# Token slots of 2112 bytes that start 64 bytes apart modulo 1024, and half the scratch for dynamic transfers

## The chip, the cores and the metric

The kernel runs on one core of one Trainium2 chip. The metric is device time in microseconds: the median of three runs, lower is better. Profile rows name the engines as PE (TensorE matmuls), PEld (TensorE weight loads), DVE (VectorE), ACT (ScalarE), POOL (GpSimd) and SP (SyncE, which issues most transfers).

## What is computed

Two transformer blocks on 256 tokens of width 2048, all in float32. The first block has two layers, each over the tokens `x` and (in layer 0, and for keys and values in layer 1) 256 context tokens:

```
hx = rmsnorm(x, norm_g[l]) * (1 + scale) + shift          # scale, shift, gate = silu(c) @ w_mod[l] + b_mod[l]
q, k, v, g_att, u_pool, g_pool, a, b, g_conv = split(hx @ w_in[l])
y  = concat(attention(q, k, v) * silu(g_att), pooling(u_pool) * silu(g_pool), conv(a, b) * silu(g_conv)) @ w_out[l]
x  = x + gate * y
```

The second block is `h @ w_in_2`, block attention, a state-space branch (64 groups of 16 channels, 64 states each) with its own `w_glu_2`, two merged branches through `w_out_2`, and a gated feed-forward part of 5632 hidden channels: `up = causal_conv3(h2 @ w_up_2)`, `x + g2 * ((silu(gt) * val) @ w_down_2)`. The output is 256 by 2048.

## The kernel before, in words

**Arithmetic.** Every large matrix product is made of three TensorE matmuls in the type float32r: each operand is split into a high part that float32r holds exactly and a low part that is the rest, and the product is high times high, high times low and low times high. All of these go through `mm` (line 152) and appear as L153. Transposes (`tr`, L159) and the small products of attention, state space and modulation are float32 matmuls, their outputs are named `sd`; outputs of the large products are named `mm`.

**Weights.** A weight chunk is 512 rows by 512 columns, 1 MB. SP loads it into a buffer `wr` (three of them, 8 KB of each partition, four k tiles of 512 columns); `_split_job` (line 352) turns it into `wh` by ACT (L168) and `wl` by DVE (L172), two buffers each. Modulation weights go through four buffers `mv` of 4 KB per partition, and in the start phase through token slots (line 852, 128 loads of 256 KB).

**Token slots.** Nearly every other tile is a token slot: `S()` (line 76) gives one of 61 buffers with tag `s`, 512 elements of 4 bytes in each partition, 2048 bytes. Split activations lie in them (high part in the first 1024 bytes and low part in the second, or one slot each), and so do attention's scores, evacuated products, rows of constants, and the pieces that POOL's queue loads and stores. `MV()`, `mid()` (tag `m`, 512 bytes), `small()` (tag `c8`) and `const()` give the other tiles.

**Who is stationary.** `chunk_a` (line 407) keeps 128 columns of a weight chunk stationary and streams the token slot past them (256 columns, or 512 in layer 0); `chunk_b` (line 384) keeps 128 tokens of a slot stationary and streams 512 weight columns. In `chunk_b` token block 0 is the slice that starts at byte 0 of the slot's half, block 1 the slice at byte 512; in `chunk_a` the stationary slice starts at byte 512 n of a 2048-byte row of the weight buffer, n from 0 to 3, and the stream at byte 0 or 1024 of the slot. `chunk_b`'s loops and matmuls:

```
order = [(b, j) for b in range(nb) for j in range(nk)]
xh, xl = lhs(kt, b)
self.mm(out, xh, hi[:, j, :], first and j == 0, False)
self.mm(out, xh, lo[:, j, :], False, False)
self.mm(out, xl, hi[:, j, :], False, end)
```

**Order.** The program is written by a planner while it is built: side tasks (attention units, the convolution, state-space preparation, modulation) are generators that `pump` (line 246) and `ensure` (line 262) step according to a running account of each engine's time, so that the order on each engine is fixed before the program runs. POOL's queue carries both arithmetic (the powers in `attn_unit`, line 1632, L218) and most transfers of less than 1 MB (`dma`, line 143, L148). For those transfers the program sets aside a scratch area at the start of every partition, 16384 bytes here.

**Places in memory.** In the built program the scratch takes bytes 0 to 16383 of a partition, constants follow, then 192 bytes named `pad`, then the token slots from byte 18432 on, then `mv`, `wr`, `wl`, `wh` from multiples of 1024. So every token slot, and every buffer of weights, starts at a multiple of 1024. The `m` tiles start 128 or 640 bytes past a multiple of 1024.

**State-space inputs.** `s5_inputs` (line 1219) loads `ssm_b_re_2` and `ssm_b_im_2` (line 1259) into one slot each, in pieces of 16 elements: 128 partitions by 32 pieces of 64 bytes, 4096 pieces a load.

Of the kernel before, what the change touches and what calls it, by code (L numbers as in the profile page):

```python
# [43 lines left out]
class Core:  # L44
# [29 lines left out]
        return f"{s}{self.uid}"  # L74

    def S(self, dt=F32, cols=512):
        return self.p.tile([128, cols], dt, tag="s", bufs=self.nslots, name=self._name("s"))

    def N(self, n, kind):

# [396 lines left out]
class Net(Core):  # L477
# [322 lines left out]
    def consts(self):  # L800
        nc, io = self.nc, self.io
        self.ident = self.const([128, 128], "ident")
        make_identity(nc, self.ident[:, :])
        self.mhalf = self.const([128, 8], "mhalf")
        nc.gpsimd.memset(self.mhalf[:, :], -0.5)
        self.mone = self.const([128, 2], "mone")
        nc.gpsimd.memset(self.mone[:, :], -1.0)
        self.ones2 = self.const([128, 2], "ones2")
        nc.gpsimd.memset(self.ones2[:, :], 1.0)
        self.mean512 = self.const([128, 1], "mean512")  # L810
        nc.gpsimd.memset(self.mean512[:, :], 1.0 / 512.0)
        self.MC = self.const([128, 16 * 12], "MC")
        self.vec1 = self.const([128, 16, 2], "vec1")
        self.vec2 = self.const([128, 16, 2], "vec2")
        self.ss0 = self.const([128, 4, 4], "ss0")
        self.const([128, 48], "pad")
        self.l1t = self.S()
        nc.gpsimd.memset(self.l1t[:, :], 0.0)
        self.MV()
        self.p.tile([128, self.KC, 512], F32, tag="wr", bufs=self.RAW, name=self._name("wr"))  # L820
        for tag in ("wl", "wh"):
            self.p.tile([128, self.KC, 512], F32R, tag=tag, bufs=2, name=self._name(tag))
        self.rows = {}
        self.mcols = {}
        self.mcn = 0
        self.sil = {}
        self.rstd = {}
# [1719 lines left out]
```

## Time and profile before

| what | value |
|---|---|
| median of 3 runs | 2958.96 us (2958.07 to 2960.7) |
| the profiled execution's own time | 2958.69 us |
| its span, first to last instruction | 2956.9 us |
| mean granted TensorE clock | 0.993 |
| PE busy | 2911.4 us, 98% of the span, 16700 matmul records |
| weight loads (PEld) | 2421.2 us, 82% |
| DVE, ACT, POOL busy | 2037.8 us, 1380.1 us, 462.6 us |
| moved by transfers | 673.44 MB, mean 228 GB/s |

A matmul's busy time in the page is longer than the distance to the next one, since matmuls are pipelined and their ends are modelled; how fast TensorE goes is read from the distance between starts. The span is 1.8 us shorter than the execution's own time.

### The profile page before, as it was taken

What the parts mean: (1) busy time and instruction counts of PE and PEld (TensorE: products, weight loads), DVE (VectorE), ACT (ScalarE), POOL (GpSimd) and SP (SyncE); (2) the same over time, 40 slices, a digit from 0 to 9 for tenths busy, and PEclk for the clock granted to TensorE, in tenths of its full rate; (3) what the DMA queues carried; (4) which work ended last, traced back from release to release, by engine and by line L of the source; (5) the groups of instructions that cost most, each with busy time, mean ns of one, the idle gap of its engine ahead of it and who ended that gap; (6) DMA issues with size and microseconds to landing.
All of it is one profiled execution on the core that took longest, in us unless ns stands there. A gap on an engine that the chain in (4) does not pass through costs nothing.

```text
span 2956.9 us, 44616 instructions
## 1 busy us (share of the span) xinstructions
PE 2911.4 (98%) x16700; PEld 2421.2 (82%) x16700; DVE 2037.8 (69%) x3703; ACT 1380.1 (47%) x3055; POOL 462.6 (16%) x915
## 2 busy tenths in 40 slices
PE   7999999999999999999998999999999999999999
PEld 4666668777788888789987888888779999999887
DVE  4447786735776689758886888778876666666544
ACT  4333223475452443466666445444455555545443
POOL 2000000343421000254225332200000000000000
PEclk9999999999999999999998999999999999999999
DMA  9768882426677553557786878898875555556564
GB/s 389 273 222 311 306 301 75 136 100 208 222 256 266 179 203 114 166 193 263 244 302 234 302 226 282 283 325 286 296 274 179 183 186 186 184 181 226 200 203 145
DMA packets 294548, 673.44 MB, mean 228 GB/s; under 512 B 22618, under 2 KB 23334, under 8 KB 294076
## 3 DMA queue, kind: packets, MB, share of 16 engines
q1 hardware_dynamic: 266240, 604.03, 59.2%
q0 software_dynamic: 23696, 59.53, 5.9%
q10 hardware_dynamic: 4396, 7.03, 0.7%
q8 instruction: 131, 2.15, 0.3%
q14 instruction: 85, 0.70, 0.1%
HBM read 643.65 MB, written 26.85 MB: 227 GB/s over the span
## 4 chain that ended last, share of the span: by engine, by line
PE 94%; DMA 2%; DVE 2%; issue 1%; ACT 1%; POOL 1%; SPq 0%; ACTq 0%; POOLq 0%; DVEq 0%
PE mm L153 83%; PE sd L153 8%; PE sd L159 3%; DVE wl L172 1%; DMA wr<-in_w_out_dram 1%; DVE s L172 0%; DVE s L192 0%; DMA s<-in_const_inv_dram 0%; ACT s L168 0%; DMA x<-in_ctx_dram 0%; DMA mv<-in_w_in_dram 0%; ACT wh L168 0%; ACT junk L168 0%; POOL s5w L148 0%; DMA s5c<-s 0%
## 5 line engine op out<-in xcount | busy, mean ns | idle before, releaser
L153 PE MATMUL mm<-wh,s 128*128 128x512 f32 x4160 | 1338.4, 395 | 2.3 <-ACT wh L168 1.4
L172 DVE TENSOR_TENSOR wl<-wr,wh 128x512 fp32r<-128x512 f32 x1480 | 924.1, 686 | 555.9 <-ACT wh L168 537.8
L168 ACT ACTIVATE wh<-wr 128x512 fp32r<-128x512 f32 x1480 | 810.6, 621 | 822.9 <-PE mm L153 636.3
L153 PE MATMUL mm<-s,wh 128*128 128x256 f32 (+1 forms) x5056 | 1054.6, 307 | 7.2 <-ACT s L168 6.9
L153 PEld LDWEIGHTS mm<-wh,s 128*128 128x128 f32 x4160 | 782.0, 188 | 192.6 <-issue 23.0
L153 PEld LDWEIGHTS mm<-s,wh 128*128 128x128 f32 x5056 | 815.5, 192 | 96.7 <-issue 48.4
L153 PE MATMUL mm<-wl,s 128*128 128x512 f32 x2080 | 811.5, 390 | 0.5 <-DVE wl L172 0.5
L153 PE MATMUL mm<-s,wl 128*128 128x256 f32 (+1 forms) x2528 | 769.0, 304 | 0.0
L153 PEld LDWEIGHTS mm<-s,wl 128*128 128x128 f32 x2528 | 486.2, 192 | 20.5 <-DVE wl L172 0.8
L153 PEld LDWEIGHTS mm<-wl,s 128*128 128x128 f32 x2080 | 391.6, 188 | 76.9 <-DVE wl L172 1.1
L192 DVE SCALAR_TENSOR_TENSOR mv<-mv,vec,mv 128x1024 f32<-128x1024 f32 x210 | 268.9, 1281 | 6.0 <-DMA mv<-in_w_mod_dram 3.6
L168 ACT ACTIVATE s<-sd 128x512 f32<-128x512 f32 (+8 forms) x298 | 114.0, 389 | 228.0 <-PE sd L159 120.9
L153 PE MATMUL sd<-s,s 128*128 128x128 f32 (+6 forms) x1248 | 180.3, 393 | 6.7 <-ACT s L168 5.0
L172 DVE TENSOR_TENSOR s<-s,s 128x256 f32<-128x256 f32 (+4 forms) x304 | 147.2, 516 | 37.6 <-ACT s L168 18.3
L168 ACT ACTIVATE s<-s 128x256 f32<-128x256 f32 (+5 forms) x312 | 129.7, 439 | 90.5 <-DVE s L172 45.7
L192 DVE SCALAR_TENSOR_TENSOR s<-s,CS,s 128x482 f32<-128x482 f32 (+30 forms) x248 | 149.2, 602 | 7.3 <-DMA s<-s5y 0.3
L153 PEld LDWEIGHTS sd<-s,s 128*128 128x128 f32 (+2 forms) x1248 | 110.5, 166 | 45.3 <-issue 24.0
L168 ACT ACTIVATE s<-mm 128x512 f32<-128x512 f32 (+1 forms) x120 | 65.4, 551 | 161.5 <-PE mm L153 159.9
L159 PE MATMUL sd<-ident,s 128*128 128x128 f32 (+1 forms) x600 | 93.4, 276 | 16.1 <-DMA s<-in_norm_g_dram 7.7
L159 PEld LDWEIGHTS sd<-ident,s 128*128 128x128 f32 (+1 forms) x600 | 73.9, 142 | 41.9 <-issue 10.7
L218 POOL TENSOR_TENSOR c<-c,mone 128x2 f32<-128x2 f32 x56 | 52.5, 938 | 270.5 <-ACT s L168 266.3
L192 DVE SCALAR_TENSOR_TENSOR s<-mm,CS,s 128x255 f32<-128x255 f32 (+1 forms) x176 | 82.5, 480 | 3.9
(210 smaller groups left out, 1577.1 us busy)
## 6 DMA issues: line engine op xcount, KB each, us to landing
wr<-in_w_in_dram SPq DMA_DIRECT2D x168, 1024.0 KB, 7.1
mv<-in_w_mod_dram SPq DMA_DIRECT2D x320, 512.0 KB, 5.4
wr<-in_w_up_dram SPq DMA_DIRECT2D x88, 1024.0 KB, 4.8
wr<-in_w_out_dram SPq DMA_DIRECT2D x48, 1024.0 KB, 8.4
wr<-in_w_down_dram SPq DMA_DIRECT2D x44, 1024.0 KB, 5.0
s<-in_w_mod_dram SPq DMA_DIRECT2D x128, 256.0 KB, 5.3
s<-s5w POOLq DMA_DIRECT2D x48, 256.0 KB, 6.3
mv<-in_w_in_dram SPq DMA_DIRECT2D x16, 512.0 KB, 6.3
```

Source lines behind the costliest of these rows:

```text
L153: self.nc.tensor.matmul(out, lhsT, rhs, start=start, stop=stop)
L159: self.nc.tensor.transpose(out, in_, self.ident[0:n, 0:n])
L168: self.nc.scalar.activation(out, in_, func, scale=scale, **kw)
L172: self.nc.vector.tensor_tensor(out, a, b, op=op)
L192: self.nc.vector.scalar_tensor_tensor(out, a, s, b, op0=op0, op1=op1)
L218: self.nc.gpsimd.tensor_tensor(out, a, b, op=op)
```

## The change

Each token slot is 528 elements wide instead of 512, so 2112 bytes, and `S()` hands out its first `cols` elements. 2112 is 2 x 1024 + 64: the first byte of each next slot lies 64 bytes further modulo 1024, and the 61 slots take all 16 such places. A second pad of 192 bytes stands behind the slots. The scratch of the dynamic transfers is 8192 bytes.

```diff
     def S(self, dt=F32, cols=512):
-        return self.p.tile([128, cols], dt, tag="s", bufs=self.nslots, name=self._name("s"))
+        return self.p.tile([128, 528], dt, tag="s", bufs=self.nslots, name=self._name("s"))[:, 0:cols]
...
         self.const([128, 48], "pad")
         self.l1t = self.S()
+        self.const([128, 48], "pad2")
         nc.gpsimd.memset(self.l1t[:, :], 0.0)
...
-    nc = _bacc.Bacc("TRN2", target_bir_lowering=False, num_devices=1)
+    nc = _bacc.Bacc("TRN2", target_bir_lowering=False, num_devices=1, dynamic_dma_scratch_size=8192)
```

In the built programs the order of the instructions on all five engines is the same row for row, 13169 rows on PE with repeats merged, and so are the semaphores that each waits for; every tile that took the k-th slot takes the k-th slot again. What differs is where things lie in a partition:

| | before | after |
|---|---|---|
| scratch | 0 to 16383 | 0 to 8191 |
| token slots | 61 of 2048 bytes from 18432 | 61 of 2112 bytes from 10240 |
| their first bytes modulo 1024 | 0 | 0, 64, 128, ... 960, then again |
| slots that start at a multiple of 256 | 61 | 16 |
| `mv`, `wr`, `wl`, `wh` from | 143360, 159744, 184320, 200704 | 139264, 155648, 180224, 196608 |
| their first bytes modulo 1024 | 0 | 0 |
| `m` tiles, first bytes modulo 1024 | 128, 640 | 128, 640 |

Behind the inserted line, line numbers are larger by one.

## Rows read from the trace of the kernel before

**Rows 1.** The page's busy times, and its granted TensorE clock in 40 slices (tenths).

```profile
PE 2911.4 (98%) x16700; PEld 2421.2 (82%) x16700; DVE 2037.8 (69%) x3703; ACT 1380.1 (47%) x3055; POOL 462.6 (16%) x915
...
PEclk9999999999999999999998999999999999999999
```

**Rows 2.** The page's chain that ended last, by engine.

```profile
PE 94%; DMA 2%; DVE 2%; issue 1%; ACT 1%; POOL 1%; SPq 0%; ACTq 0%; POOLq 0%; DVEq 0%
```

**Rows 3.** Waits of PE, whole span: us in total, times, longest.

```profile
PE sd L159 <- DMA s<-in_norm_g_dram: 7.7, 1, 7.7
PE mm L153 <- ACT s L168: 7.3, 5, 2.5
```

**Rows 4.** The page's large products: count | busy us, mean ns | idle before.

```profile
L153 PE MATMUL mm<-wh,s 128*128 128x512 f32 x4160 | 1338.4, 395 | 2.3 <-ACT wh L168 1.4
...
L153 PE MATMUL mm<-s,wh 128*128 128x256 f32 (+1 forms) x5056 | 1054.6, 307 | 7.2 <-ACT s L168 6.9
...
L153 PE MATMUL mm<-wl,s 128*128 128x512 f32 x2080 | 811.5, 390 | 0.5 <-DVE wl L172 0.5
L153 PE MATMUL mm<-s,wl 128*128 128x256 f32 (+1 forms) x2528 | 769.0, 304 | 0.0
```

**Rows 5.** Windows, feed-forward: length, busy PE, PEld, DVE, ACT, POOL, clock, DMA, GB/s.

```profile
2400.00:2700.00 300.00, 300.00 (x2502) 300.00 (x2501) 192.97 (x361) 156.27 (x309) 3.23 (x6) 1.00 0.55 187
```

**Rows 6.** PE's timeline in the down projection: start, length in us.

```profile
2800.47 0.39 PE L153 MATMUL mm<-wl,s 128*128 128x512 f32 x1
...
2801.15 0.39 PE L153 MATMUL mm<-wl,s 128*128 128x512 f32 x1
...
2802.51 0.39 PE L153 MATMUL mm<-wl,s 128*128 128x512 f32 x1
...
2803.19 0.39 PE L153 MATMUL mm<-wl,s 128*128 128x512 f32 x1
```

**Rows 7.** DVE's groups by line and form.

```profile
L172 DVE TENSOR_TENSOR s<-s,s 128x512 f32<-128x512 f32 x72 | 49.6, 692 | 3.6 <-ACT s L168 1.5
...
L172 DVE TENSOR_TENSOR s<-mm,s 128x512 f32<-128x512 f32 x56 | 38.4, 687 | 25.9 <-PE mm L153 19.3 <-ACT s L168 6.4
```

**Rows 8.** Windows of the start phase, columns as in Rows 5.

```profile
20.00:80.00 60.00, 57.34 (x300) 32.21 (x301) 27.46 (x73) 22.52 (x48) 5.40 (x10) 0.97 1.05 404
80.00:140.00 60.00, 60.00 (x306) 38.44 (x306) 24.43 (x58) 22.22 (x42) 0.00 (x0) 1.00 0.73 246
```

**Rows 9.** Loads of modulation weights into slots between 20 and 80 us.

```profile
L852 SPq DMA_DIRECT2D s<-in_w_mod_dram x68: 327/328/1125, 20.1 to 79.3; - x68
```

**Rows 10.** Transfers by line: issuing queue, count, KB each, median us to landing.

```profile
s<-in_w_mod_dram SPq DMA_DIRECT2D x128, 256.0 KB, 5.3
...
s<-s5u POOLq DMA_DIRECT2D x32, 32.0 KB, 5.2
...
m<-in_w_pool_dram POOLq DMA_DIRECT2D x8, 64.0 KB, 4.5
...
s<-in_ssm_b_re_dram POOLq DMA_DIRECT2D x1, 256.0 KB, 7.1
s<-in_ssm_b_im_dram POOLq DMA_DIRECT2D x1, 256.0 KB, 8.6
```

**Rows 11.** POOL's timeline around the two loads of line 1259.

```profile
543.13 1.73 POOL L148 DMA_DIRECT2D s<-in_ssm_b_re_dram  x1
544.84 1.70 POOL L148 DMA_DIRECT2D s<-in_ssm_b_im_dram  x1
...
552.36 0.19 POOL L218 TENSOR_TENSOR c<-c,neglam 128x1 f32<-128x1 f32 x1
```

**Rows 12.** DVE's timeline behind them.

```profile
558.55 2.73 DVE L192 SCALAR_TENSOR_TENSOR s<-s,c,s 128x512 f32<-128x512 f32 x4
561.20 0.75 DVE L172 TENSOR_TENSOR s<-s,s5p 128x256 f32<-128x256 f32 x2
```

**Rows 13.** PE's timeline behind them.

```profile
562.03 1.04 PE L159 MATMUL sd<-ident,s 128*128 128x128 f32 x8
```

## The prediction

> **What bounds the kernel now.** Three views, in this order. The page's busy times say which engine is short of time: PE is busy 2911.4 of 2956.9 us, so all its idle time together is 45.5 us [rows 1]. The chain of work that ended last says the same of the path: 94% of it is PE, 2% transfers, 2% DVE, 1% ACT [rows 2]. The waits of PE say that nothing single stands in its way: the longest is 7.7 us for the first load of columns, and all waits of the large products for ACT's work on slots come to 7.3 us [rows 3]. So the time is the number of matmuls times the distance between them, and the distance is the number to look at. A matmul's busy time (395 ns, 307 ns in the groups [rows 4]) is not that distance, because matmuls overlap. In the stretch from 2400 to 2700 us, where 256 columns stream past each set of weights, 2502 matmuls start in 300.00 us: 119.9 ns each [rows 5]. In the down projection, where 512 columns stream, three matmuls take 2801.15 - 2800.47 = 0.68 us: 227 ns each [rows 6]. The granted clock is 1.00 in the first stretch, which is the 2.4 GHz level [rows 5], and 9 or more tenths in all but one slice of the span, which has 8 [rows 1]. From 256 to 512 columns the distance grows by 107 ns, which is 2.4 columns a nanosecond. So a matmul takes its columns at full clock (106.7 or 213.3 ns) and about 13 ns on top, whatever its length. The four groups of large products hold 4160 + 5056 + 2080 + 2528 = 13824 matmuls [rows 4]; their 13 ns make 13824 x 13.3 ns = 184 us. That is all that an address could give back on this engine.
>
> **The change, part by part.** The program's instructions, their order on each engine, the waits and the slot that each tile takes stay as they are. So no instruction is added or removed, and this term is 0 exactly. Left are the effects of where slots lie and of the smaller scratch.
>
> *Matmuls that read a slot and a weight buffer together.* If the two reads collide in some way that depends on their distance modulo 1024, the 13 ns could be the collision. Before, two distances occur: 0 and 512. In the down projection the 12 matmuls of token block 0 hold weights from byte 0 of a slot's half, and the 12 of block 1 from byte 512, against the same stream of weight columns. Block 0 goes from 2800.47 to 2801.15, block 1 from 2802.51 to 2803.19: 0.68 us for three, both times [rows 6]. In the stretch at 256 columns the stationary slice starts at 0, 512, 1024 and 1536 in turn, and the mean is 119.9 ns with DVE busy 192.97 and ACT 156.27 of the 300 us on slots and weights [rows 5]. So neither a shift by half the period nor other engines' traffic moves the distance. The 61 new places bring distances of 64, 128 and so on, that no large product has had; the row nearest to them is the one at 512, and it says 0. I take 0. The ends are -184 us (all of the 13 ns was collision) and, with no row that excludes a loss, as much upwards for a collision that the present places avoid.
>
> *DVE and ACT on slots.* A DVE operation that reads two slots, both at a multiple of 1024, takes 692 ns on 512 columns; with one input from PSUM it takes 687 ns [rows 7]. If the 5 ns are a collision of the two reads, it is 0.7% of such an operation. PE's whole idle time is 45.5 us [rows 1], so at most 0.3 us of it can go. I take 0. The split of weights into `wh` and `wl`, DVE's largest group, touches no slot.
>
> *Transfers into slots.* In the start phase modulation weights come through slots: 128 loads of 256 KB [rows 10], 68 of them between 20 and 80 us [rows 9], where the transfer engines' share is 1.05 at 404 GB/s, so they have nothing to spare [rows 8]. One load takes 262144 B / 404 GB/s = 0.65 us there. After the change 45 of 61 slots start off a multiple of 256. If a row of 2048 bytes then costs nine blocks of 256 where it cost eight, a load is 0.081 us longer; 68 x 0.081 x 45/61 = 4.1 us for the full stretch, and 7.7 us if all 128 pay and PE follows every one. Against a cost: the `m` tiles start 128 past a multiple of 256 already, and 64 KB land in them in 4.5 us where 32 KB into aligned slots take 5.2 us [rows 10]. And PE is busy 57.34 of those 60 us and all 60 of the next [rows 8], so a late load must first use up its lead. I take 0, with 0 and +7.7 us as ends. The Trainium skill's page "DMA: Bandwidth & Descriptors", section "How a descriptor splits into AXI transactions", speaks against the change here: a read that does not start at a multiple of 256 bytes begins at the boundary below and pays for the bytes ahead of it. It says this of reads; no run here shows it for writes into slots, and by it as it stands only stores out of slots would grow.
>
> *Half the scratch.* The scratch serves POOL's transfers. The two loads of line 1259 are by far the most cut up, 4096 pieces each, 256 for each of 16 transfer engines; their issue takes 1.73 and 1.70 us [rows 11]. If the smaller scratch cannot hold both, the second waits until the first has landed, 543.13 + 7.1 = 550.2 us instead of 544.84, so POOL is 5.4 us late [rows 10, 11]. Behind them stand the powers of four attention units; the last ends at 552.55, so 557.95 at the latest [rows 11]. DVE takes their results up at 558.55, since it has a weight split to do first, and PE turns them at 562.03 [rows 12, 13]. The second load itself would land by 550.2 + 8.6 = 558.8, and DVE reads it from 561.20 on [rows 10, 12]. So the delay ends before anyone waits: I take 0; 5.4 us is the price if the cover were gone. The Trainium skill's same page, sections "Terms" and "The descriptor swizzle", gives 16 bytes to a descriptor and one closing descriptor to each engine's share. An estimate by it: 8192 / 16 = 512 places, and 2 x 257 do not fit, so the wait would come; no run here shows it yet.
>
> **The sum** is 0 against the profiled execution's own time of 2958.69 us. The median of the runs is 0.27 us above that, so I forecast 2959.0 us. About 0.2%, 5.9 us, can be told from no change.
>
> **The rivals.** *Slower, by late slot loads:* the nine-block price above, at the start phase. It gives 2963 to 2967 us (4.1 to 7.7). It decides as soon as loads come later than PE's own work in 20 to 80 us covers. For it: a share of 1.05 [rows 8]. Against: the `m` tiles. *Scratch wait uncovered:* up to 2964.4 us; the margins above, 0.6 us on DVE, are thin. *Faster, reads collide less:* the 13 ns shrink. All of it would give 2775 us, half 2867 us. For it: the constant is there and unexplained by the columns. Against: the equal distances at 0 and 512. *Slower, reads collide more:* multiples of 512 may be the good case; a tenth of the constant more on each matmul is 18 us, 2977 us. Against: nothing but the same two rows. That the slots don't move as said is excluded, the built program's places show it.
>
> **How the numbers follow.** The forecast has 0.64. Late slot loads have 0.13, of which 0.08 is over 0.2%; the uncovered scratch wait 0.05, 0.01 of it over; fewer collisions 0.11, all faster; more collisions 0.07, all slower. Faster 0.11; same 0.64 + 0.05 + 0.04 = 0.73; slower 0.08 + 0.01 + 0.07 = 0.16. The range leaves out both collision cases (0.18): from 2953 us, a little below the lowest run with some room for another chip, to 2967 us, the end of the late loads.
>
> **What would show it.** Right: 0.68 us for three matmuls in the down projection and 2502 in 300 us of the feed-forward stretch, for slots of all places alike; 692 ns still on DVE; the windows of the start phase within 1 us. The scratch wait would show as an issue of the second load of line 1259 that lasts 7 us instead of 1.70, with DVE's four combinations still near 558.55. Wrong: a new distance between matmuls, different for different slots; a start phase that lasts 4 us or more longer; a wait of PE behind POOL near 560 us.

## The result and the profile after

The changed kernel takes **2974.63 us** (median of three runs, 2973.74 to 2976.61) against 2958.96 us: ratio 1.0057, 95% interval 1.0043 to 1.0071. It is slower by 15.7 us, and the forecast of no change was wrong. The profiled execution's span is 2974.8 us against 2956.9 us, 17.9 us more.

The page's busy times, its granted clock and its chain:

```profile
PE 2929.1 (98%) x16700; PEld 2412.2 (81%) x16700; DVE 2037.0 (68%) x3703; ACT 1380.7 (46%) x3055; POOL 464.8 (16%) x915
...
PEclk9999999999999999999998999999999999999999
...
PE 94%; DMA 2%; DVE 1%; issue 1%; ACT 1%; POOL 1%; SPq 0%; ACTq 0%; POOLq 0%; DVEq 0%
```

PE is busy 2929.1 us, 17.7 us more than before [rows 1]; its idle time is 45.7 us where it was 45.5. The row of the granted clock reads as before, and PE's share of the chain is 94% again [rows 1, 2]. So PE does not wait longer, it works longer, on the same 16700 matmuls. Its waits say the same (us in total, times, longest):

```profile
PE mm L153 <- ACT s L168: 8.5, 5, 2.5
PE sd L159 <- DMA s<-in_norm_g_dram: 8.2, 1, 8.2
```

Together 1.7 us more than the same two rows before [rows 3]. The large products:

```profile
L153 PE MATMUL mm<-wh,s 128*128 128x512 f32 x4160 | 1354.9, 399 | 2.7 <-ACT s L168 1.6
...
L153 PE MATMUL mm<-s,wh 128*128 128x256 f32 (+1 forms) x5056 | 1046.2, 306 | 7.2 <-ACT s L168 6.9
...
L153 PE MATMUL mm<-wl,s 128*128 128x512 f32 x2080 | 819.0, 394 | 0.5 <-DVE wl L172 0.5
L153 PE MATMUL mm<-s,wl 128*128 128x256 f32 (+1 forms) x2528 | 765.0, 303 | 0.2 <-DVE wl L172 0.2
```

The two groups with 512 weight columns (`wh,s` and `wl,s`) grew by 16.5 and 7.5 us, the two with 256 columns, which hold the 1392 streams of layer 0 too, shrank by 8.4 and 4.0 us [rows 4]. Two opposite effects, then. The same stretch of the feed-forward product as in [rows 5], 20 us later because the program runs later (window, length, busy time and count of PE, PEld, DVE, ACT, POOL, clock, DMA share, GB/s):

```profile
2420.00:2720.00 300.00, 300.00 (x2535) 300.00 (x2534) 195.12 (x365) 157.80 (x312) 4.37 (x9) 1.00 0.56 191
```

2535 matmuls in 300 us, 118.3 ns each, where 2502 took 119.9. That part has become faster. In the down projection the trace holds its own comparison, because its last eight stationary tiles lie in `mv` buffers, which still start at multiples of 1024, and the others in slots. PE's timeline across the border (start, length in us; rows of two overlapping matmuls are left out, each row here is the second of its three):

```profile
2844.84 0.39 PE L153 MATMUL mm<-wl,mv 128*128 128x512 f32 x1
...
2845.52 0.39 PE L153 MATMUL mm<-wl,mv 128*128 128x512 f32 x1
...
2846.20 0.39 PE L153 MATMUL mm<-wl,mv 128*128 128x512 f32 x1
...
2848.24 0.39 PE L153 MATMUL mm<-wl,s 128*128 128x512 f32 x1
...
2848.94 0.40 PE L153 MATMUL mm<-wl,s 128*128 128x512 f32 x1
...
2849.64 0.39 PE L153 MATMUL mm<-wl,s 128*128 128x512 f32 x1
```

With stationary operands from `mv` three matmuls take 2845.52 - 2844.84 = 0.68 us, as before [rows 6]. From 2848 us on they come from slots, and three take 0.70 us. Averaged over each kind, from the start of one matmul to the next, where the matmuls before and after are large products too and no wait lies between (the column of matmuls counts all of the kind):

| stream past stationary | matmuls | before | after |
|---|---|---|---|
| 512 weight columns past a slot | 6240 | 227.5 ns | 231.6 ns |
| 512 columns of a slot past weights (layer 0) | 1392 | 229.1 ns | 231.3 ns |
| 256 columns of a slot past weights | 6192 | 119.95 ns | 118.32 ns |

6240 x 4.1 + 1392 x 2.2 - 6192 x 1.63 = 25.6 + 3.1 - 10.1 = 18.6 us, against 17.9 us in the spans. The pace of the matmuls accounts for the whole result, to within 0.7 us. Matched matmul by matmul, the changed kernel is 0.7 us late at 156 us, 14.1 at 1355, 20.2 at 2206, then gains in the feed-forward product to 13.8 at 2711, and loses again in the down projection to 17.9.

### The profile page after: what moved, and what is told of

Its sections match the earlier page's. It is cut to its first block, busy times and chain, and to the rows that moved or that the text cites. A ratio compares the mean times of both kernels' runs of the same rounds, so it can differ in the third digit from the quotient of the medians.

```text
span 2974.8 us, 44616 instructions
## 1 busy us (share of the span) xinstructions
PE 2929.1 (98%) x16700; PEld 2412.2 (81%) x16700; DVE 2037.0 (68%) x3703; ACT 1380.7 (46%) x3055; POOL 464.8 (16%) x915
## 4 chain that ended last, share of the span: by engine, by line
PE 94%; DMA 2%; DVE 1%; issue 1%; ACT 1%; POOL 1%; SPq 0%; ACTq 0%; POOLq 0%; DVEq 0%
PE mm L153 83%; PE sd L153 8%; PE sd L159 3%; DMA wr<-in_w_out_dram 1%; DVE wl L172 0%; ACT s L168 0%; DMA wr<-in_w_in_dram 0%; DMA x<-in_ctx_dram 0%; DVE s L192 0%; DMA mv<-in_w_in_dram 0%; ACT wh L168 0%; DVE s L172 0%; ACT junk L168 0%; POOL s5w L148 0%; DMA s5c<-s 0%
## 5 line engine op out<-in xcount | busy, mean ns | idle before, releaser
L153 PE MATMUL mm<-wh,s 128*128 128x512 f32 x4160 | 1354.9, 399 | 2.7 <-ACT s L168 1.6
L153 PEld LDWEIGHTS mm<-s,wh 128*128 128x128 f32 x5056 | 805.3, 190 | 98.6 <-issue 48.7
L153 PEld LDWEIGHTS mm<-s,wl 128*128 128x128 f32 x2528 | 478.6, 189 | 21.2 <-DVE wl L172 0.9
L159 PE MATMUL sd<-ident,s 128*128 128x128 f32 (+1 forms) x600 | 93.5, 276 | 16.5 <-DMA s<-in_norm_g_dram 8.2
```

What stands on the lines that cost most here:

```text
L153: self.nc.tensor.matmul(out, lhsT, rhs, start=start, stop=stop)
L159: self.nc.tensor.transpose(out, in_, self.ident[0:n, 0:n])
```

## The experiments

Three theories of the pace were tried against one of the transfers. **Distance:** what counts is how many bytes lie between the stream's first byte and the stationary operand's, modulo some period. **Place:** a slot that does not stand at a multiple of 512 is slow by itself. **Mixture:** the pace is lost when successive matmuls read from different places. Against them: the smaller **scratch** or the loads into shifted slots.

### The scratch alone

```diff
-    nc = _bacc.Bacc("TRN2", target_bir_lowering=False, num_devices=1)
+    nc = _bacc.Bacc("TRN2", target_bir_lowering=False, num_devices=1, dynamic_dma_scratch_size=8192)
```

> Only the smaller scratch; slots of 2048 bytes, all at a multiple of 1024. Pace theories (mixture, distance, place): as before, 2959 us within 0.2%, three 512-column matmuls of the down projection still 0.68 us; POOL's second load of line 1259 still waits some 8 us, and PE does not notice. Scratch theory: a good part of the 15.7 us, so above 2965 us.

Measured: 2958.65 us, ratio 0.9998 (0.9989 to 1.0008). POOL's timeline at the two loads:

```profile
543.21 1.74 POOL L148 DMA_DIRECT2D s<-in_ssm_b_re_dram  x1 [0.82 <-issue]
551.95 1.70 POOL L148 DMA_DIRECT2D s<-in_ssm_b_im_dram  x1 [7.00 <-issue]
```

The second load waits 7.00 us. Behind it DVE waits 0.43 us for POOL's last power, and PE has no wait from 545 to 600 us. The scratch costs nothing that shows in the time. The windows of this kernel serve as the measure for those below: 200 us of the feed-forward product and 150 us of the down projection, columns as above. A count holds one or two matmuls at the edges.

```profile
2420.00:2620.00 200.00, 200.00 (x1669) 200.00 (x1668) 128.21 (x240) 103.73 (x206) 0.00 (x0) 1.00 0.55 183
2750.00:2900.00 150.00, 150.00 (x663) 124.21 (x662) 77.72 (x124) 61.55 (x112) 0.00 (x0) 1.00 0.61 204
```

### All slots 64 bytes further

```diff
-        self.const([128, 48], "pad")
+        self.const([128, 64], "pad")
         self.l1t = self.S()
+        self.const([128, 240], "pad2")
```

Slots stay 2048 bytes long, at 64 modulo 1024; scratch 8 KB, here and in all versions of the kernel that follow.

> Slots of 2048 bytes again, but all of them 64 bytes past a multiple of 1024; weights and mv stay on multiples of 1024; scratch 8 KB. Mixture theory (the pace is lost when successive matmuls read from different places modulo 1024): within a chunk all places are equal again, so 2959 us within 0.2%. Distance theory (slot against weight buffer in one matmul) and place theory (slot not at a multiple of 512): the loss stays or grows, 2970 to 2985 us, with some 231 to 233 ns for 512 columns and some 118 ns for 256.

Measured: 2979.67 us, ratio 1.0054 (1.0033 to 1.0075), but in two clusters: three executions at 2963.2 to 2963.8, five at 2979.5 to 2980.6 us. The profiled one is of the lower cluster:

```profile
2420.00:2620.00 200.00, 200.00 (x1767) 200.00 (x1766) 133.77 (x252) 109.02 (x216) 0.00 (x0) 1.00 0.58 193
2750.00:2900.00 150.00, 150.00 (x648) 121.54 (x647) 75.19 (x120) 59.34 (x108) 0.00 (x0) 1.00 0.59 197
```

The down projection is slower than with the slots at 0 (648 for 663) and the feed-forward product much faster (1767 for 1669: 113.3 ns). (Part of the matmuls in the down projection's window hold tiles from `mv`, which did not move, and stay at 227 ns.) All slots have one place here, so mixture alone cannot be the cause. A pace of 113.3 ns was not expected by any theory. With it the sum is 6240 x 5.8 + 1392 x 0.7 - 6192 x 5.4 = +3.7 us, close to the 5.1 us of the spans; the upper cluster, which was not profiled, stands 16.5 us above; the 4224 matmuls of the feed-forward product would cost 19 us more at 117.8 ns (that pace comes up in the maps).

### Slots, `mv` and weights all 64 bytes further

```diff
-        self.const([128, 48], "pad")
+        self.const([128, 64], "pad")
```

> Slots, mv, wr, wl and wh all start 64 bytes past a multiple of 1024, so that the distance between slot and weights is a multiple of 512 as before; scratch 8 KB. Distance theory: 2959 us within 0.2%, 227 ns for 512 columns. Place theory: as slow as with the slots alone shifted or slower, above 2970 us. Mixture theory: 2959 us too.

Measured: 2960.57 us, ratio 1.0007 (0.9998 to 1.0016).

```profile
2420.00:2620.00 200.00, 200.00 (x1669) 200.00 (x1669) 127.88 (x240) 103.92 (x206) 0.00 (x0) 1.00 0.55 183
2750.00:2900.00 150.00, 150.00 (x664) 124.24 (x663) 77.70 (x124) 61.20 (x112) 0.00 (x0) 1.00 0.61 204
```

Both paces are back, with these buffers all off a multiple of 256. Place falls for the matmuls. For transfers it shows no cost in the time: all loads of weights land 64 bytes off here, and the time is that of before. Distance stands.

### A map of distances

```python
for i in range(rep):
    a = 512 * (i % 8) + w[i % len(w)] // 4
    b = 1024 * (i % 4) + m[i % len(m)] // 4
    nc.tensor.matmul(ps[bank][:, 0:n], W[:, a:a + 128], M[:, b:b + n], start=i == 0, stop=i == rep - 1)
```

> Nothing of the reference is computed: float32r matmuls on zeros, 30 in a row for each pair of places, 512 and 256 columns, the stationary operand at w and the stream at m bytes past a multiple of 1024, on a grid of 64 bytes and some finer and coarser places; the whole set twice, the second time in reverse order. Distance theory: the pace depends on m - w alone, 227 and 120 ns where it is 0 or 512. Place theory: it depends on w or on m by itself. Mixture theory: 227 and 120 ns for each constant pair, and another pace only in the sequences that change place from matmul to matmul.

Mean ns from start to start over the last 20 of a stretch's 29 intervals, from the trace, second pass; rows w, columns m in bytes. Where the two passes differ by over a nanosecond both are given, the first one first. The rest of the grid, up to 448 for both, repeats this block with a period of 256 in either direction, up to which of two paces stands where there are two.

| 512 columns, w | m 0 | 64 | 128 | 192 |
|---|---|---|---|---|
| 0 | 226.8 | 228.9 | 232.6 | 233.3 |
| 64 | 233.3 | 226.8 | 228.9 | 232.6 |
| 128 | 232.6 | 233.3 | 226.9 | 228.8 |
| 192 | 228.9 | 232.6 | 233.3 | 226.9 |

| 256 columns, w | m 0 | 64 | 128 | 192 |
|---|---|---|---|---|
| 0 | 120.0 | 117.8 | 118.7 | 113.3 |
| 64 | 117.8, 113.3 | 120.0 | 113.3, 117.8 | 118.7 |
| 128 | 118.7 | 113.3 | 120.0 | 117.8 |
| 192 | 117.8 | 118.7 | 113.3 | 120.0 |

The diagonals are constant: on this grid the pace depends on m - w modulo 256, on nothing else of the place. 0 is the best distance for 512 columns and the worst for 256. Distances of 64 and 192 have two settled paces at 256 columns, 113.3 and 117.8 ns; at 512 columns each of the four distances has one. (The 120 matmuls at distance 0 that open the run are not in the table: their first twelve intervals are 388 to 591 ns long, then they settle on 226.7 too.) Of the finer places, w = 16, a distance of -16, showed 226.7 in the first pass and 233.4 in the second. The sequences that pass through eight places came to 231.0 to 232.3 ns for 512 columns, where the mean of the four distances is 230.4: mixture adds something, and a later run looks at that.

### A finer map, with other beginnings

> Nothing of the reference is computed: float32r matmuls on zeros in the kernel's own pattern (high times high, high times low, low times high, four stationary slices in turn), stream minus stationary from -128 to 120 bytes in steps of 8; each stretch of 36 begins behind the one before, behind four float32 matmuls, or behind six matmuls of the other length. Distance theory with a period of 256: 512 columns have their best at 0 (227 ns) and lose up to 7 ns elsewhere; 256 columns are worst at 0 (120 ns) and lie between 113 and 119 elsewhere. If 113 and 118 ns are two settled paces of the same distance, the beginning decides between them and the same distance shows both.

Mean ns of the last 18 intervals, behind the stretch before / behind float32 matmuls / behind the other length; a choice of the 32 distances:

| m - w | 512 columns | 256 columns |
|---|---|---|
| -64 | 233.3 / 233.3 / 233.3 | 113.3 / 113.3 / 113.3 |
| -32 | 233.3 / 233.3 / 233.3 | 118.4 / 118.3 / 118.5 |
| -16 | 236.7 / 236.7 / 236.7 | 117.0 / 117.4 / 117.2 |
| 0 | 226.7 / 226.7 / 226.7 | 120.0 / 120.0 / 120.0 |
| 8 | 232.2 / 232.2 / 233.3 | 120.0 / 126.7 / 120.0 |
| 64 | 228.9 / 228.9 / 228.9 | 117.8 / 117.8 / 117.8 |
| 112 | 231.1 / 231.1 / 231.1 | 113.3 / 113.3 / 113.3 |
| -128 | 233.3 / 233.3 / 232.5 | 120.0 / 118.8 / 120.0 |

For 512 columns 0 is the best distance here; the next best of the 32 is 64, 2.2 ns worse. At -16 this map shows 236.7 ns, where the first one, with another order of slices, showed 226.7 and 233.4, so that off the steps of 64 bytes a distance does not fix the pace. At 48 of the 64 settings the beginning changed the mean by no more than 1 ns, at the other 16 by 1.1 to 10.1 ns. At -64 and 64 it did not bring out the second pace, against the expectation.

### The 512-column products alone

```diff
         self.index[key] = len(self.jobs)
+        if key[0] in ("o", "ab", "sb", "dn") or key[0] == "g" and key[2][0] in "qkvs":
+            self.narrow.add(len(self.jobs))
...
+    def half(self, tag, i):
+        o = self.OFF if i in self.narrow else 0
+        t = self.p.tile([128, 2048 + 64], F32R, tag=tag, bufs=2, name=self._name(tag))
+        return t[:, o:o + 2048].rearrange("p (k n) -> p k n", n=512)
+
+    OFF = 48
...
-        hi = self.p.tile([128, self.KC, 512], F32R, tag="wh", bufs=2, name=self._name("wh"))
-        lo = self.p.tile([128, self.KC, 512], F32R, tag="wl", bufs=2, name=self._name("wl"))
+        hi, lo = self.half("wh", i), self.half("wl", i)
...
```

> Slots at multiples of 1024; only the chunks whose 512 weight columns stream past stationary tokens lie 192 bytes further in wh and wl (6432 matmuls), all else stays at distance 0; scratch 8 KB. Distance theory, by the map: those go from 227.5 to 233.3 ns, +37 us, 2996 us; 256 columns stay at 120.0 and the streams of layer 0 at 229. Mixture theory: within a product nothing alternates, so 2959 us. If the loss came from slots that stand off 256 for transfers, ACT or DVE: 2959 us.

Measured: 2991.66 us, ratio 1.0113 (1.0099 to 1.0127), 33.5 us over the runs beside it where 37 were expected.

```profile
2420.00:2620.00 200.00, 200.00 (x1669) 200.00 (x1668) 129.75 (x245) 104.85 (x209) 0.00 (x0) 1.00 0.55 183
2750.00:2900.00 150.00, 150.00 (x645) 120.21 (x644) 71.80 (x117) 59.10 (x108) 0.00 (x0) 1.00 0.58 197
```

The paces are the map's (233.3 ns, 120.0 ns); the counts fall from 663 to 645 in the one window and stay at 1669 in the other. The slots are where they were before, and moving the weights against them is enough. That is the loss of the change, in a larger dose. In the profiled execution, whose span is 29.9 us above that of the kernel before, the intervals of the moved products that hold no wait and have no small product beside them grew by 35.8 us, and the 390 beside a small product did not grow. Everything else together shrank by 5.9 us, most of it in waits between large products.

### The 256-column products alone

As the last diff, with `OFF = 16` (64 bytes) and the condition `key[0] in ("val", "gt", "glu") or key[:2] == ("g", 1) and key[2][0] not in "qkv" or key[:2] == ("g", 2) and key[2][0] == "u"`, which marks the chunks that 256 columns stream past.

> Slots of 2048 bytes at multiples of 1024; the buffers wh and wl are 256 bytes longer, and the chunks that stream 256 columns lie 64 bytes further in them, so that stream minus stationary is -64 there and 0 in all products of 512 columns; scratch 8 KB. Distance theory, by the map: 512 columns stay at 227 ns, 256 columns go from 120.0 to 113.3 ns (7584 of them: 50 us, 2908 us) or to 117.8 (17 us, 2941 us), or one of them in one execution and the other in another. Mixture and place theories: no gain, 2959 us or more.

Measured: 2923.99 us, ratio 0.9887 (0.9866 to 0.9908), executions from 2919.0 to 2938.5. The 7584 in the expectation was a miscount: 1392 of them are the 512-column streams of layer 0, so 6192 x 6.7 = 41 us, 2917 us. The profiled execution is the slowest of the five:

```profile
2420.00:2620.00 200.00, 200.00 (x1700) 200.00 (x1699) 131.76 (x250) 107.78 (x216) 0.00 (x0) 1.00 0.57 188
2750.00:2900.00 150.00, 150.00 (x664) 124.20 (x663) 75.41 (x122) 60.01 (x110) 0.00 (x0) 1.00 0.60 203
```

117.8 ns in the feed-forward product. Run once more:

> The run with 64 bytes once more, to see how the executions spread. 6192 matmuls at 113.3 instead of 120.0 ns give 2917 us, at 117.8 ns 2945 us; with the feed-forward part (4224 of them) on the one or the other pace for a whole execution, two clusters some 19 us apart, near 2920 and 2938 us. If the first run's spread was chance of another kind, no gap between them.

Measured: 2923.52 us, ratio 0.9897 (0.9878 to 0.9916); five executions at 2922.5 to 2925.3 us, one at 2941.9. Profiled from the lower cluster:

```profile
2420.00:2620.00 200.00, 200.00 (x1767) 200.00 (x1766) 137.35 (x260) 111.08 (x220) 0.00 (x0) 1.00 0.59 195
2750.00:2900.00 150.00, 150.00 (x664) 124.20 (x663) 73.17 (x117) 59.56 (x109) 0.00 (x0) 1.00 0.58 197
```

113.3 ns there, and 113.8 over all 256-column products: 6192 x 6.1 = 37.8 us, against 36.0 us between the spans. So there are the two clusters, and this version is faster than both kernels in every one of its eleven executions.

The same with `OFF = 36`, a distance of -144, which is 112 modulo 256:

> As the run with 64 bytes, but the chunks that stream 256 columns lie 144 bytes further, so that stream minus stationary is 112 modulo 256 (6192 matmuls). By the fine map this distance and -64 are the two that settled at 113.3 ns from every beginning: 6192 x 6.7 = 41 us, 2918 us, and 2932 to 2945 us where the kernel's own interruptions settle it on another pace. If the gain were one of -64 alone, 2959 us.

Measured: 2957.43 us, ratio 0.9992 (0.9980 to 1.0003), one of twelve executions at 2941.4.

```profile
2420.00:2620.00 200.00, 200.00 (x1669) 200.00 (x1669) 128.40 (x241) 103.74 (x206) 0.00 (x0) 1.00 0.55 183
2750.00:2900.00 150.00, 150.00 (x663) 124.21 (x662) 77.23 (x124) 61.50 (x112) 0.00 (x0) 1.00 0.60 204
```

120.0 ns, a miss: what the quiet map gave at 112 from three beginnings the kernel does not reach. Whether it settles on another pace of the same distance, or whether -144 is not the same as 112, is open: the period of 256 was seen in steps of 64 bytes alone, and no map stood at -144. On those steps a map gives the paces that a distance can settle on; which of them a kernel settles on it does not tell.

### Slots of 2176 bytes

```diff
-        return self.p.tile([128, cols], dt, tag="s", bufs=self.nslots, name=self._name("s"))
+        return self.p.tile([128, 544], dt, tag="s", bufs=self.nslots, name=self._name("s"))[:, 0:cols]
...
         self.l1t = self.S()
+        self.const([128, 96], "pad2")
```

> Slots of 2176 bytes, 128 apart modulo 1024, scratch 8 KB. Distance theory with a period of 256: half of the slots at distance 0, half at 128. 512 columns: (227.5 + 232.6) / 2 = 230.0 ns, 2.5 more on 6240 matmuls, +15.8 us; 256 columns: (120.0 + 118.7) / 2 = 119.35, -4.6 us; together 2969 us. If the period were 128, 2959 us; if 512 or more, or if only the number of places counted, nearer to the 2975 us of 16 places.

Measured: 2979.37 us, ratio 1.0065 (1.0050 to 1.0081): 10 us more than by distance.

```profile
2420.00:2620.00 200.00, 200.00 (x1682) 200.00 (x1682) 130.35 (x246) 106.05 (x212) 0.00 (x0) 1.00 0.56 185
2750.00:2900.00 150.00, 150.00 (x651) 122.17 (x650) 72.92 (x118) 59.57 (x109) 0.00 (x0) 1.00 0.58 197
```

Averaged as in the table above, 512 columns past a slot take 231.6 ns, not 230.0. Two places are as bad as sixteen, so either distance is not all, or the mean over a mixture is not the mean of its parts.

### Distances that change

> Nothing of the reference is computed: 144 float32r matmuls on zeros for each setting, as in the fine map, but with a distance of stream and stationary that changes every 1, 3, 6, 12 or 24 matmuls, between 0 and 128, 0 and 64, or through 0, 64, 128, 192 in two orders. Distance theory alone: the mean of the constant paces whatever the hold, for 512 columns 229.7 (0 and 128), 227.8 (0 and 64), 230.4 (all four); for 256 columns 119.4, 118.9 and 117 to 119. If changes cost something of their own, which the run with 128 byte steps hints at (232.1 instead of 230.0), the mean rises as the hold gets shorter, by 1 to 3 ns at a change in every third matmul, and goes to the constant paces' mean at 24.

Windows of 32 us at 512 columns (constant 0, 64, 128, 192; then 0 and 128, and 0 and 64, changing at every third matmul), then of 16 us at 256 columns (constant 0, 64, 128, 192):

```profile
52.75:84.75 32.00, 32.00 (x143) 26.50 (x142) 0.00 (x0) 0.00 (x0) 1.00 0.00 1
85.39:117.39 32.00, 32.00 (x141) 26.28 (x140) 0.00 (x0) 0.00 (x0) 1.00 0.00 1
118.37:150.37 32.00, 32.00 (x139) 25.98 (x138) 0.00 (x0) 0.00 (x0) 1.00 0.00 1
151.83:183.83 32.00, 32.00 (x139) 25.79 (x138) 0.00 (x0) 0.00 (x0) 1.00 0.00 1
218.87:250.87 32.00, 32.00 (x140) 25.95 (x139) 0.00 (x0) 0.00 (x0) 1.00 0.00 1
385.04:417.04 32.00, 32.00 (x139) 25.91 (x138) 0.00 (x0) 0.00 (x0) 1.00 0.00 1
849.49:865.49 16.00, 16.00 (x136) 16.00 (x135) 0.00 (x0) 0.00 (x0) 1.00 0.00 1
866.77:882.77 16.00, 16.00 (x139) 16.00 (x137) 0.00 (x0) 0.00 (x0) 1.00 0.00 1
883.73:899.73 16.00, 16.00 (x137) 16.00 (x136) 0.00 (x0) 0.00 (x0) 1.00 0.01 1
900.82:916.82 16.00, 16.00 (x139) 16.00 (x138) 0.00 (x0) 0.00 (x0) 1.00 0.00 1
```

Counts of 143, 141, 139 and 139 for the constant distances, and 140 and 139 for the two mixtures, where halves of 143 and 139 or 141 would give 141 and 142. In ns from the starts: 231.8 for 0 and 128 (the parts' mean is 229.5), 232.2 for 0 and 64 (227.8), 231.3 and 231.7 for all four in two orders (230.3). With a hold of 24 matmuls the same settings come to 230.7, 228.0, 230.3 and 231.1. At 256 columns and a hold of 3 all four give 118.3 and 118.9 ns (118.6). So at 512 columns and changes at every third matmul, changing costs 1.0 to 4.4 ns on top of the parts' mean. It is not even: 0 and 64 with a hold of 6 or 12 show 227.8, the mean itself, and all four distances with a hold of 6 show 232.1 and 231.7. (The 232.1 in the expectation is too high for the run that it speaks of: that mean is 231.6.) In this kernel the slot changes with every third matmul, in layer 0 more often. The changed kernel shows 231.6 beside the 231.3 to 231.7 of the map, and the slots of 2176 bytes show 231.6 beside its 231.8. So the paces of the two kernels with mixed slots agree with the map; that their order of distances is that of the map was not read off, and in so far it is argued.

## Why the prediction was wrong

**The bound was read rightly.** PE sets the time, by the distance between its matmuls; the 15.7 us came by that way. The instructions and their order did not matter, as said.

**The step that failed is the term for matmuls that read a slot and a weight buffer together: "the row nearest to them is the one at 512, and it says 0. I take 0".** The rows at 0 and 512 are one case, not two: by the map the pace has, in steps of 64 bytes, a period of 256 bytes, so every large product of the kernel before stood at distance 0. Their agreement said only that 512 is a multiple of the period. Nearness in bytes was taken for nearness in effect. Distances of 64, 128 and 192 had no row. The ends of 184 us to either side were all that the trace allowed, and the 0 between them had no support. What was put at 0 measured 25.6 + 3.1 - 10.1 = 18.6 us: more on the products of 512 columns, less on those of 256.

**The 13 ns were read as one constant "whatever its length".** They are what distance 0 gives at both lengths. At 64, 128 and 192 the 256 columns take 113.3 to 118.7 ns, which is 6.6 to 12.0 ns over the 106.7 of the columns, and 512 columns take 228.9 to 233.3, 15.6 to 20 over 213.3.

**The rivals.** "Slower, reads collide more: multiples of 512 may be the good case" had 0.07, and its price of 18 us and 2977 us came within 3 us of the result. Its working was a guess that came out well: not a tenth more on each matmul, but 4.1 ns on 6240, 2.2 on 1392 and 1.63 less on 6192. "Faster, reads collide less" is true of the 256-column products (10 us), and of the version with the weights moved by 64 bytes (34 us). The range left both collision cases out; with a support of nothing but one distance, they deserved more than 0.18 together.

**DVE and ACT: right.** ACT is busy 1380.7 us where it was 1380.1. DVE's 692 and 687 ns [rows 7] are now

```profile
L172 DVE TENSOR_TENSOR s<-s,s 128x512 f32<-128x512 f32 x72 | 49.5, 691 | 3.7 <-ACT s L168 1.5
...
L172 DVE TENSOR_TENSOR s<-mm,s 128x512 f32<-128x512 f32 x56 | 38.4, 687 | 29.0 <-PE mm L153 22.5 <-ACT s L168 6.6
```

**Loads into slots: right.** The two windows of the start phase [rows 8] with slots off 256:

```profile
20.00:80.00 60.00, 57.34 (x299) 31.90 (x300) 27.48 (x73) 22.50 (x48) 5.44 (x10) 0.97 1.05 400
80.00:140.00 60.00, 60.00 (x305) 38.19 (x305) 23.93 (x57) 21.73 (x42) 0.00 (x0) 1.00 0.72 248
```

One matmul record fewer in each, in the first the same share of 1.05 and 400 for 404 GB/s; the changed kernel is 0.7 us late at 156 us, where the nine-block price wanted 4.1 to 7.7, and the kernel with all buffers off 256 runs at 2960.57 us. The rival of late loads falls.

**Half the scratch: right in the time, though the wait looks otherwise than announced and is longer.** POOL's two loads, and the first one's time to landing (us, last column):

```profile
548.46 1.73 POOL L148 DMA_DIRECT2D s<-in_ssm_b_re_dram  x1 [0.82 <-PE sd L153]
556.35 1.70 POOL L148 DMA_DIRECT2D s<-in_ssm_b_im_dram  x1 [6.16 <-ACT s L168]
```

```profile
s<-in_ssm_b_re_dram POOLq DMA_DIRECT2D x1, 256.0 KB, 7.5
```

The second is issued at 556.35, just behind the first one's landing at 548.46 + 7.5 = 555.96, where it followed after 1.71 us before [rows 11]. The profile shows the wait as idle time ahead of an issue of 1.70 us and names ACT as its releaser; it is not a longer issue, as I had written. The estimate by the Trainium skill's page "DMA: Bandwidth & Descriptors" (sections "Terms" and "The descriptor swizzle"), that the two do not fit into 8192 bytes together, agrees with this 6.16 us and with the 7.00 us of the kernel with the scratch alone. With the scratch alone POOL's second load is 551.95 - 544.84 = 7.1 us late and not 5.4, since the first one took 8.3 us to land and not 7.1. The cover held, with 0.43 us of DVE waiting: that kernel is at 0.9998.

## What to carry to other kernels

Where float32r matmuls set the time, measure the pace at several distances between stream and stationary operand, as one would for any other parameter, and place buffers by it: here distance 0 modulo 256 for 512 columns, and 64 bytes off for 256 columns, which is 1.0% of this kernel for 64 columns of padding in four buffers. Rows that agree are evidence only if they differ in what may matter; a kernel whose buffers all start at multiples of 512 has one sample. Staggering the slots did not help here, and at 512 columns a distance that changes with every third matmul cost more than its parts.

## What the runs showed of the hardware that was not expected

- The pace of these float32r matmuls, each with its own weight load, depends in steps of 64 bytes on m - w modulo 256 bytes: 226.7, 228.9, 232.6, 233.3 ns at 0, 64, 128, 192 for 512 columns, and 120.0, 117.8 or 113.3, 118.7, 113.3 or 117.8 ns for 256, at a granted clock of 1.00. Why is open: no run looks into the engine.
- A stream of matmuls can stay on one of two paces of the same distance for a whole stage of 480 us, and the executions of one program then fall into clusters 16 to 19 us apart (2963 and 2980 us, of which the lower was profiled; 2923 and 2942 us, of which both were). One execution can hold both paces: in the slower profiled one with the weights moved by 64 bytes, the 256-column products between 1560 and 2050 us took 113.6 ns in the mean, and the feed-forward product behind them 117.8. What decides is open too: three kinds of beginning in the fine map did not bring it out.
